# Fox attention pairs taken from the middle outwards, both score buffers in one pool, and the u and y transposes issued in halves

## The chip, the cores and the metric

The kernel runs on one core of one Trainium2 chip. The metric is device time in microseconds (us): the median of several executions. One more execution was taken with the hardware profiler, and every row below is from that one. TensorE is called PE (its weight loads PEld), VectorE DVE, ScalarE ACT, GpSimd POOL, and SP is the queue that issues most DMAs.

## The reference

Two residual layers over x [1, 2048, 1024] and a final RMSNorm, all float32. The part that the change touches most is the forgetting attention (FoX) of layer 0, eight heads of 64, in blocks of 128 queries:

```python
def one_block(args):
    i, qi, ci = args
    s = jnp.einsum('bhqd,bhkd->bhqk', qi, k, preferred_element_type=F32) * scale
    s = s + ci[..., :, None] - c[..., None, :]          # c = cumsum(log f)
    s = jnp.where(kpos[None, :] <= qpos[:, None], s, -jnp.inf)
    p = jax.nn.softmax(s, axis=-1)
    return jnp.einsum('bhqk,bhkd->bhqd', p.astype(v.dtype), v)
```

Around it, in each layer: `u = rmsnorm(h)`, `z = u @ w_in`, a second mixer (gated linear attention, GLA, in layer 0; retention and a dilated attention in layer 1), and `h + (mix * silu(gate)) @ w_out`.

## The kernel before

Nearly every product is done three times with float16 halves (high by high, high by low, low by high), so each operand is split into a high part (ACT, line 84) and a low part (DVE, line 85). The program runs through five stages.

1. **u** (0 to 130 us). For each of 16 tiles of 128 rows, `put_u` squares x on ACT with the junk result going into the low half of `u_x`, makes 1/rms (DVE, POOL), splits into `u_x` (two buffers), and one DMA transpose on SP writes both halves into `ut` (line 101). Beside it PE projects head 0.
2. **Fox** (130 to 1070 us). `periods` runs heads 0 to 7. While head h attends, PE is given the projection of head h+1 (`Heads.tiles`, four row tiles at a time, then one DMA transpose per quarter of the sequence, line 414) and other projections as fill; `merge` mixes both lists by cost, and `issue_after` keeps the value products behind the fill that was put ahead of them.
3. **Even mix** (1070 to 1372 us): `mix_out` with GLA recurrence beside it; it splits y and transposes it (line 322), multiplies by w_out, and makes u of the next layer.
4. **Dilated attention** (1372 to 2180 us).
5. **Odd mix** (2180 to 2489 us), with retention.

A pair step n of the Fox stage works on the query blocks 15-n and n, always 17 blocks of keys together. `scores` (lines 482 to 524): PE makes the scores in up to three PSUM tiles `big` (two buffers; lines 501 to 504), DVE adds the decay row `cb` and takes the maximum into `fx_s` (line 506), ACT takes the exponential in place (514) and copies the high half to `fx_ph` (518), DVE writes the low half back into `fx_s` (519), and SP issues two DMA transposes, `fx_ph` to `fx_th` (522) and `fx_s` to `fx_tl` (523). `values` follows two steps later (LAG): PE multiplies `fx_th` and `fx_tl` by v (533, 534), DVE scales (539), POOL adds the halves (545) and stores each group of four blocks (548). The last two value steps of a head run early in the next head's list. `decay` loads the two halves of `cb` per head by broadcast DMAs on SP (478) into three buffers, and POOL scales them (479).

`fx_s` has two buffers, one in the Fox pool for even n and one in the pool `wq` of the projection weights for odd n; when `start_gla` closes that pool during head 7, a single one is left (lines 485 and 486). The pool of the GLA is opened on the space of `wq`.

All engines run their queues in order. The framework writes the order of the queues at build time from its own estimate (line 1215) and puts in every wait.

Of the kernel before, what the change touches and what calls it, by code (L numbers as in the profile page):

```python
# [7 lines left out]
F32 = mybir.dt.float32  # L8
# [28 lines left out]
class Core:  # L37
# [52 lines left out]
    def put_u(self, u, t, h, work):  # L90

        nc = self.nc
        b, j = divmod(t, 4)
        if j == 0:
            u[b] = self.upool.tile([128, 2, KT, 512], F16, name="ut")
        x = work.tile([128, 2, D], F16, name="u_x", bufs=U_BUFS)
        ssq = self.small.tile([128, 1], F32, name="ssq")
        nc.scalar.activation(x[:, 1].bitcast(BF16), h, AF.Square, accum_out=ssq)
        r = self.rstd(ssq, D, 10)
        self.split(x[:, 0], x[:, 1], h, r[:, 0:1])  # L100
        nc.sync.dma_start_transpose(u[b].rearrange("p s k n -> p (s k) n")[:, :, j * 128:(j + 1) * 128],
                                    x.rearrange("p s n -> p (s n)"))
# [51 lines left out]
    def rows(self, out, u, t, w, c0, c1):  # L154
# [3 lines left out]
        uh, ul = u[b][:, 0], u[b][:, 1]  # L158
# [7 lines left out]
    def cols(self, out, u, b, w, c0, c1):  # L166

        nc = self.nc
        uh, ul = u[b][:, 0], u[b][:, 1]
# [120 lines left out]
def mix_out(co, work, inputs, h_d, gate_d, gate_k, kept_d, first, ws, recur, finish, lag):  # L290
# [13 lines left out]
    def prep(t):  # L304
# [8 lines left out]
        x = inputs.tile([128, 2, D], F16, name="u_x", bufs=U_BUFS)  # L313
        hi, lo = x[:, 0], x[:, 1]
# [6 lines left out]
        yt = work.tile([128, 2, KT, 128], F16, name="yt", bufs=lag + 1)  # L321
        nc.sync.dma_start_transpose(yt.rearrange("p s k n -> p (s k) n"), x.rearrange("p s n -> p (s n)"))
        ys[t] = (yt[:, 0], yt[:, 1], inv, h)
# [32 lines left out]
class Heads:  # L356
# [5 lines left out]
    def __init__(self, co, pools, xpool, wpool, u, w_in, col0, gain, chunked, rope=None):  # L362
# [4 lines left out]
        self.wpool_closed = False  # L367
# [95 lines left out]
def fox(co, work, heads, cum_d, mix_d, causal):  # L463
# [18 lines left out]
    def scores(h, n):  # L482

        st, f, cb = heads.st[h], heads.f[h], cbs[h]
        pool = work if n % 2 == 0 or heads.wpool_closed else heads.wpool
        raw = pool.tile([128, 2 * W], F16, name="fx_s", bufs=1)
# [29 lines left out]
        ph = work.tile([128, W], F16, name="fx_ph")  # L516
# [9 lines left out]
    def values(h, n):  # L526
# [11 lines left out]
        o2 = work.tile([128, 2, 128], F32, name="fx_o2")  # L538
        nc.vector.tensor_mul(o2, pv, nm[:, 6:8, None].to_broadcast([128, 2, 128]))  # L539
        for part, i in enumerate((15 - n, n)):  # L540
            g = i // 4
            if (h, g) not in outs:
                outs[h, g] = [work.tile([128, 4, 64], F32, name="fx_o", bufs=3), 0]
# [123 lines left out]
def gla(co, work, glq_d, glv_d, tables, gm):  # L667
# [307 lines left out]
def decoder(tc, cst, x, norm_even, w_in_even, b_f_even, w_lr_even, b_lr_even, gla_norm_even, w_out_even,  # L975
            norm_odd, w_in_odd, ret_gn_w_odd, ret_gn_b_odd, w_out_odd, final_norm, out):
    nc = tc.nc
    with ExitStack() as ctx:
# [240 lines left out]
```

## Time and profile before

| | |
|---|---|
| median of 3 runs | 2489.22 us (2487.48 to 2505.09) |
| the profiled execution's own time | 2491.33 us |
| its span, first to last instruction | 2489.5 us |
| TensorE busy, share of the span | 2231.9 us, 90% |
| DVE, ACT, POOL busy | 1562.9, 1122.8, 535.1 us |
| mean granted TensorE clock | 0.938 of full |

The median of the runs and the profiled execution differ by 0.1%. The page of the profile gives shares over the whole span; the stages have different limits, so waits are read stage by stage. A clock of 1.0 is the 2.4 GHz level, 0.5 the 1.2 GHz level.

### The profile page before, as it was taken

The numbers are of one execution on the slowest core, as the hardware profiler recorded it, in microseconds if no ns is written. First come the engines' busy times: TensorE is split into PE (matmuls) and PEld (weight loads), VectorE is DVE, ScalarE is ACT, GpSimd is POOL, SyncE is SP. The second block draws the span as 40 slices with busy tenths as digits, with TensorE's granted clock in tenths as the row PEclk, the third lists the DMA queues.
The fourth block names the chain that finished last, engine by engine and source line by source line (L and its number), as shares of the span: only waits on it lengthen the run. The fifth ranks groups of instructions, "written<-read, shape, count | busy, mean of one in ns | idle before, by whom it ended". The sixth has DMA issues, their size and how long they took to land. (4 is left out here: it accounts for less than half of the span.)

```text
span 2489.5 us, 51410 instructions
## 1 busy us (share of the span) xinstructions
PE 2231.9 (90%) x19956; PEld 1717.4 (69%) x19956; DVE 1562.9 (63%) x4870; ACT 1122.8 (45%) x2580; POOL 535.1 (21%) x638
## 2 busy tenths in 40 slices
PE   4888789998898898768989999999998999889998
PEld 3777678576687787534445898898887888765554
DVE  5346557576575665445554866666665757688764
ACT  5445445454444443334343555455554545533332
POOL 0021221201112112111111222212312222154441
PEclk8799899999999999869999999999999999989999
DMA  9848787888787756568776677886858667866553
GB/s 198 182 102 151 142 153 151 149 147 154 144 165 139 144 115 149 106 192 186 202 182 160 143 152 144 134 156 143 172 113 149 148 136 153 162 212 180 167 155 102
DMA packets 838452, 381.85 MB, mean 153 GB/s; under 512 B 741040, under 2 KB 797248, under 8 KB 837952
## 3 DMA queue, kind: packets, MB, share of 16 engines
q1 hardware_dynamic: 740784, 259.28, 53.9%
q0 software_dynamic: 23584, 82.33, 11.8%
q10 hardware_dynamic: 73840, 36.97, 6.0%
q8 instruction: 156, 2.56, 0.4%
q14 instruction: 88, 0.72, 0.1%
HBM read 135.40 MB, written 73.73 MB: 84 GB/s over the span
## 5 line engine op out<-in xcount | busy, mean ns | idle before, releaser
L162 PE MATMUL dn<-w,ut 128*128 128x192 f16 (+1 forms) x3840 | 1014.4, 264 | 24.8 <-DMA ut<-u_x 10.0
L163 PE MATMUL dn<-w,ut 128*128 128x192 f16 (+1 forms) x3840 | 1013.3, 264 | 0.0
L164 PE MATMUL dn<-w,ut 128*128 128x192 f16 (+1 forms) x3840 | 1012.6, 264 | 0.0
L162 PEld LDWEIGHTS <-ut 128*128 128x128 f16 x3968 | 395.6, 100 | 65.5 <-DMA ut<-u_x 29.3
L163 PEld LDWEIGHTS <-ut 128*128 128x128 f16 x3968 | 395.0, 100 | 39.3 <-issue 10.4
L164 PEld LDWEIGHTS <-ut 128*128 128x128 f16 x3968 | 394.8, 100 | 27.3 <-issue 1.4
L506 DVE CUSTOM_DVE_ANT_0 fx_s<-big,cb,hd_f 128x1024 f32<-128x1024 f32 (+7 forms) x128 | 134.1, 1048 | 173.7 <-DMA fx_tl<-fx_s 90.3
L514 ACT ACTIVATE fx_s<-fx_s,fx_nm 128x2048 f32<-128x2048 f32 (+15 forms) x128 | 152.7, 1194 | 194.0 <-DVE fx_nm L512 193.9
L897 ACT ACTIVATE dl_s<-dl_s,dl_m 128x256 f32<-128x256 f32 (+1 forms) x384 | 172.6, 451 | 107.0 <-DVE dl_m L896 93.0
L519 DVE TENSOR_TENSOR fx_s<-fx_s,fx_ph 128x2176 f16<-128x2176 f32 x64 | 155.0, 2422 | 38.4 <-ACT fx_ph L518 38.3
L501 PE MATMUL big<-head 128*128 128x512 f16 (+3 forms) x320 | 119.1, 372 | 59.9 <-DMA head<-qk_x 36.8
L893 DVE CUSTOM_DVE_ANT_0 dl_s<-big,dl_mask,hd_f 128x256 f32<-128x256 f32 (+1 forms) x384 | 141.5, 421 | 47.6 <-PE big L891 46.7
L79 POOL TENSOR_TENSOR rs_r<-rs_v,mhalf 128x1 f32<-128x1 f32 (+2 forms) x96 | 69.5, 727 | 427.4 <-DVE rs_v L76 407.0
L900 DVE TENSOR_TENSOR dl_pl<-dl_s,dl_ph 128x512 f16<-128x512 f32 (+2 forms) x96 | 101.4, 1058 | 66.2 <-ACT dl_ph L899 44.0
L533 PE MATMUL aux<-head,fx_th 128*128 128x128 f16 x1088 | 115.3, 227 | 25.0 <-DMA fx_th<-fx_ph 25.0
L85 DVE SCALAR_TENSOR_TENSOR w<-w_raw,w_gs,w 128x256 f16<-128x256 f32 (+2 forms) x296 | 123.1, 472 | 14.7 <-ACT w L84 14.5
L518 ACT ACTIVATE fx_ph<-fx_s 128x2176 f16<-128x2176 f32 x64 | 128.8, 2012 | 5.3 <-issue 3.3
L891 PE MATMUL big<-head 128*128 128x256 f16 (+1 forms) x384 | 129.7, 357 | 0.9 <-DMA head<-qk_x 0.9
L890 PE MATMUL big<-head 128*128 128x256 f16 (+1 forms) x384 | 129.6, 355 | 0.6 <-DVE dl_rec L893 0.6
L84 ACT ACTIVATE w<-w_raw,w_gs 128x256 f16<-128x256 f32 (+2 forms) x296 | 113.6, 466 | 32.8 <-DVE w_gs L143 24.0
L545 POOL TENSOR_TENSOR fx_o<-fx_o 128x64 f32<-128x64 f32 x128 | 52.9, 433 | 344.7 <-DVE fx_o L539 211.6
L534 PE MATMUL aux<-head,fx_tl 128*128 128x64 f16 x1088 | 110.1, 199 | 16.0 <-DMA fx_tl<-fx_s 15.9
(235 smaller groups left out, 4387.0 us busy)
## 6 DMA issues: line engine op xcount, KB each, us to landing
gate_d<-x_out POOLq DMA_DIRECT2D x64, 256.0 KB, 4.4
o_gate<-gate_d SPq DMA_DIRECT2D x32, 512.0 KB, 5.2
rec_d<-dl_rec POOLq DMA_DIRECT2D x16, 528.0 KB, 4.7
dl_rec<-rec_d POOLq DMA_DIRECT2D x16, 528.0 KB, 5.9
x_h<-in_x_dram SPq DMA_DIRECT2D x16, 512.0 KB, 4.8
cb<-cum_d SPq DMA_DIRECT2D x16, 512.0 KB, 9.5
o_mix<-mix_d SPq DMA_DIRECT2D x32, 256.0 KB, 2.8
o_h<-in_x_dram SPq DMA_DIRECT2D x16, 512.0 KB, 5.1
```

Of the source, the lines that this page charges most:

```text
L85: self.nc.vector.scalar_tensor_tensor(lo, x, scale, hi, op0=OP.mult, op1=OP.subtract)
L162: nc.tensor.matmul(out, uh[:, k, xs], wh[:, k, c0:c1], start=k == 0, stop=False)
L163: nc.tensor.matmul(out, uh[:, k, xs], wl[:, k, c0:c1], start=False, stop=False)
L164: self.last = nc.tensor.matmul(out, ul[:, k, xs], wh[:, k, c0:c1], start=False, stop=k == KT - 1)
L506: nc.vector.tensor_tensor_reduce(out=x[:, at + c * 1024:at + c * 1024 + wide], in0=p[:, :wide], in1=cb[c][:, :wide], scale=f[:, 0:1], scal ...
L514: nc.scalar.activation(x[:, sp], x[:, sp], AF.Exp, bias=nm[:, part:part + 1], accum_out=nm[:, 2 + part:3 + part])
L518: nc.scalar.activation(ph, x[:, 0:W], AF.Copy)
L519: nc.vector.tensor_sub(pl, x[:, 0:W], ph)
L890: nc.tensor.matmul(p[:, sp], st[:, 0, qs], st[:, 1, ks], start=True, stop=False)
L891: nc.tensor.matmul(p[:, sp], st[:, 0, qs], st[:, 2, ks], start=False, stop=True)
L893: nc.vector.tensor_tensor_reduce(out=raw[:, sp], in0=p[:, sp], in1=mask[:, 256 - 128 * len(vs):], scale=f[:, 0:1], scalar=-3.0e38, op0=OP. ...
L897: nc.scalar.activation(raw[:, sp], raw[:, sp], AF.Exp, bias=m[:, i:i + 1], accum_out=rec[:, n, 65:66])
```

## The change

Four things. Fox pairs are taken from n = 7 to n = 0, so the first pair of a head is (8, 7) and the last (15, 0). Both `fx_s` buffers are in the Fox pool for the whole stage; to make room `fx_ph` and `fx_o2` go from two buffers to one, `fx_o` from three to two, and the GLA's `gl_ek` from four to three. The high and low halves of u, and of y, are tiles of their own, each with a DMA transpose of its own (twice as many, half as wide). The query and key transposes of a head's quarter (line 414) stay one DMA, as before.

```diff
@@ put_u @@
-            u[b] = self.upool.tile([128, 2, KT, 512], F16, name="ut")
-        x = work.tile([128, 2, D], F16, name="u_x", bufs=U_BUFS)
+            u[b] = (self.upool.tile([128, KT, 512], F16, name="uh"),
+                    self.upool.tile([128, KT, 512], F16, name="ul"))
+        hi = work.tile([128, D], F16, name="u_hi", bufs=U_BUFS)
+        lo = work.tile([128, D], F16, name="u_lo", bufs=U_BUFS)
...
-        nc.sync.dma_start_transpose(u[b].rearrange("p s k n -> p (s k) n")[:, :, j * 128:(j + 1) * 128],
-                                    x.rearrange("p s n -> p (s n)"))
+        for part, x in zip(u[b], (hi, lo)):
+            nc.sync.dma_start_transpose(part[:, :, j * 128:(j + 1) * 128], x)
@@ mix_out, prep @@
-        yt = work.tile([128, 2, KT, 128], F16, name="yt", bufs=lag + 1)
-        nc.sync.dma_start_transpose(yt.rearrange("p s k n -> p (s k) n"), x.rearrange("p s n -> p (s n)"))
+        yh = work.tile([128, KT, 128], F16, name="yh", bufs=lag + 1)
+        yl = work.tile([128, KT, 128], F16, name="yl", bufs=lag + 1)
+        nc.sync.dma_start_transpose(yh, hi)
+        nc.sync.dma_start_transpose(yl, lo)
@@ fox @@
-        pool = work if n % 2 == 0 or heads.wpool_closed else heads.wpool
-        raw = pool.tile([128, 2 * W], F16, name="fx_s", bufs=1)
+        raw = work.tile([128, 2 * W], F16, name="fx_s")
...
-        ph = work.tile([128, W], F16, name="fx_ph")
+        ph = work.tile([128, W], F16, name="fx_ph", bufs=1)
...
-        o2 = work.tile([128, 2, 128], F32, name="fx_o2")
+        o2 = work.tile([128, 2, 128], F32, name="fx_o2", bufs=1)
...
-                outs[h, g] = [work.tile([128, 4, 64], F32, name="fx_o", bufs=3), 0]
+                outs[h, g] = [work.tile([128, 4, 64], F32, name="fx_o", bufs=2), 0]
...
-        steps = [(1.9, lambda n=n: scores(h, n), 1.5, lambda n=n: behind(h, n)) for n in range(8)]
+        steps = [(1.9, lambda n=n: scores(h, n), 1.5, lambda n=n: behind(h, n)) for n in range(7, -1, -1)]
@@ gla @@
-                ek = work.tile([128, 128], F32, name="gl_ek", bufs=4)
+                ek = work.tile([128, 128], F32, name="gl_ek", bufs=3)
```

## Rows read from the trace of the kernel before

**Rows 1.** The page's first line: the span.

```profile
span 2489.5 us, 51410 instructions
```

**Rows 2.** Busy time by stretch (start:end, length, then busy us of PE, PEld, DVE, ACT, POOL with instruction counts, granted clock, DMA share, GB/s): the Fox stage, the even mix, the dilated stage.

```profile
170.00:1070.00 900.00, 796.85 (x8027) 638.09 (x8026) 557.02 (x1292) 411.51 (x664) 165.82 (x240) 0.94 0.75 144
1110.00:1372.00 262.00, 238.66 (x1250) 124.84 (x1248) 141.83 (x435) 104.94 (x275) 36.57 (x58) 0.95 0.73 180
1372.00:2180.00 808.00, 771.47 (x7844) 682.64 (x7842) 547.49 (x2270) 419.51 (x1288) 192.67 (x206) 0.97 0.75 147
```

**Rows 3.** What PE waited for from 130 to 1070 us: us in total, times, longest.

```profile
PE big L501 <- DMA head<-qk_x: 36.8, 6, 9.4
PE aux L533 <- DMA fx_th<-fx_ph: 25.0, 7, 5.8
...
PE aux L534 <- DMA fx_tl<-fx_s: 15.9, 13, 3.2
```

**Rows 4.** Timeline of PE: the first score product of heads 4, 5 and 7 (three of the six waits); start, us, engine, line, shape, count, and in brackets the idle time before it and its releaser.

```profile
569.98 0.61 PE L501 MATMUL big<-head 128*128 128x512 f16 x1 [9.38 <-DMA head<-qk_x]
670.65 0.61 PE L501 MATMUL big<-head 128*128 128x512 f16 x1 [6.74 <-DMA head<-qk_x]
872.46 0.61 PE L501 MATMUL big<-head 128*128 128x512 f16 x1 [5.78 <-DMA head<-qk_x]
```

**Rows 5.** Busy time by stretch, the sum line over the six stretches of half clock that follow or span the six waits (360.4 to 367.3, 466.2 to 469.7, 565.2 to 575.5, 667.6 to 674.5, 766.6 to 773.4, 869 to 875.8 us).

```profile
sum 41.20, PE 25.24 PEld 10.05 DVE 11.27 ACT 0.00 POOL 12.47; mean PE 4.21 PEld 1.68 DVE 1.88 ACT 0.00 POOL 2.08
```

**Rows 6.** DVE: its waits for the score buffer from 130 to 1070 us, and on its timeline the first reduction of the second pair of heads 2, 3, 6 and 7.

```profile
DVE fx_s L506 <- DMA fx_tl<-fx_s: 90.3, 23, 9.7
...
374.37 1.28 DVE L506 CUSTOM_DVE_ANT_0 fx_s<-big,cb,hd_f 128x1024 f32<-128x1024 f32 x1 [3.50 <-DMA fx_tl<-fx_s]
478.16 1.28 DVE L506 CUSTOM_DVE_ANT_0 fx_s<-big,cb,hd_f 128x1024 f32<-128x1024 f32 x1 [5.52 <-DMA fx_tl<-fx_s]
783.56 1.28 DVE L506 CUSTOM_DVE_ANT_0 fx_s<-big,cb,hd_f 128x1024 f32<-128x1024 f32 x1 [5.45 <-DMA fx_tl<-fx_s]
888.65 1.28 DVE L506 CUSTOM_DVE_ANT_0 fx_s<-big,cb,hd_f 128x1024 f32<-128x1024 f32 x1
```

**Rows 7.** Timeline of the SP queue where head 1 ends and head 2 begins (the second number is the time that the issue took).

```profile
346.76 0.36 SPq L478 DMA_DIRECT2D cb<-cum_d  x1
347.30 7.72 SPq L522 DMA_TRANSPOSE fx_th<-fx_ph  x1
355.12 3.11 SPq L523 DMA_TRANSPOSE fx_tl<-fx_s  x1
...
359.84 0.90 SPq L478 DMA_DIRECT2D cb<-cum_d  x1
360.90 8.73 SPq L522 DMA_TRANSPOSE fx_th<-fx_ph  x1
369.73 2.39 SPq L523 DMA_TRANSPOSE fx_tl<-fx_s  x1
```

**Rows 8.** Where head 0 ends and head 1 begins: two copies to `fx_ph` on ACT's timeline, and two first value products on PE's.

```profile
252.17 2.00 ACT L518 ACTIVATE fx_ph<-fx_s 128x2176 f16<-128x2176 f32 x1
265.13 2.02 ACT L518 ACTIVATE fx_ph<-fx_s 128x2176 f16<-128x2176 f32 x1
...
255.99 0.29 PE L533 MATMUL aux<-head,fx_th 128*128 128x128 f16 x1 [5.45 <-DMA fx_th<-fx_ph]
271.25 0.23 PE L533 MATMUL aux<-head,fx_th 128*128 128x128 f16 x1 [3.87 <-DMA fx_th<-fx_ph]
```

**Rows 9.** The last pair of head 7: its first reduction on DVE's timeline, its first value product on PE's.

```profile
1043.51 1.28 DVE L506 CUSTOM_DVE_ANT_0 fx_s<-big,cb,hd_f 128x1024 f32<-128x1024 f32 x1 [6.04 <-DMA fx_tl<-fx_s]
...
1059.19 0.29 PE L533 MATMUL aux<-head,fx_th 128*128 128x128 f16 x1 [5.76 <-DMA fx_th<-fx_ph]
```

**Rows 10.** DMA transposes: issue time on SP (ns, shortest/median/longest, first and last start) of u (2048 columns; the first stage alone) and of the dilated stage (512 to 1024 columns), then the median us from issue to landing of the same two.

```profile
L101 SPq DMA_TRANSPOSE ut<-u_x x16: 1317/2612/4720, 13.5 to 105.3; - x16
...
L901 SPq DMA_TRANSPOSE dl_pt<-dl_ph x96: 1188/1232/3942, 1402.7 to 2159.8; - x96
...
dl_pt<-dl_ph SPq DMA_TRANSPOSE x96, 3.6
...
ut<-u_x SPq DMA_TRANSPOSE x32, 4.4
```

**Rows 11.** The u stage: PE's waits for transposed u (0 to 170 us), busy time of two stretches, and the projections' matmuls over the whole run (ns, first and last start).

```profile
PE aux L162 <- DMA ut<-u_x: 13.8, 7, 3.5
PE dn L162 <- DMA ut<-u_x: 10.0, 3, 3.7
...
0.00:107.00 107.00, 65.06 (x727) 54.57 (x728) 55.68 (x162) 53.52 (x101) 9.00 (x20) 0.81 0.95 202
107.00:130.00 23.00, 23.00 (x225) 19.45 (x222) 8.93 (x24) 12.67 (x21) 1.65 (x2) 0.93 0.50 99
...
L162 PE MATMUL dn<-w,ut x3840: 242/264/421, 17.9 to 2211.1; 128*128 128x192 f16 x106, 128*128 128x256 f16 x86
```

**Rows 12.** From Fox to the even mix: DVE's wait for weights of the next layer, the first read-back of a mixed tile on SP, and the stores of Fox outputs on POOL (ns, first and last start).

```profile
DVE w_am L131 <- DMA w_raw<-in_w_in_odd_dram: 10.3, 1, 10.3
...
1067.02 0.32 SPq L301 DMA_DIRECT2D o_mix<-mix_d  x1
...
L548 POOL DMA_DIRECT2D mix_d<-fx_o x32: 750/767/825, 225.3 to 1066.9; - x32
```

More of the change, by code (lines that the diff above doesn't have):

```diff
@@ L94, in put_u @@
         if j == 0:
-            u[b] = self.upool.tile([128, 2, KT, 512], F16, name="ut")
-        x = work.tile([128, 2, D], F16, name="u_x", bufs=U_BUFS)
+            u[b] = (self.upool.tile([128, KT, 512], F16, name="uh"),
+                    self.upool.tile([128, KT, 512], F16, name="ul"))
+        hi = work.tile([128, D], F16, name="u_hi", bufs=U_BUFS)
+        lo = work.tile([128, D], F16, name="u_lo", bufs=U_BUFS)
         ssq = self.small.tile([128, 1], F32, name="ssq")
-        nc.scalar.activation(x[:, 1].bitcast(BF16), h, AF.Square, accum_out=ssq)
+        nc.scalar.activation(lo.bitcast(BF16), h, AF.Square, accum_out=ssq)
         r = self.rstd(ssq, D, 10)
-        self.split(x[:, 0], x[:, 1], h, r[:, 0:1])
-        nc.sync.dma_start_transpose(u[b].rearrange("p s k n -> p (s k) n")[:, :, j * 128:(j + 1) * 128],
-                                    x.rearrange("p s n -> p (s n)"))
+        self.split(hi, lo, h, r[:, 0:1])
+        for part, x in zip(u[b], (hi, lo)):
+            nc.sync.dma_start_transpose(part[:, :, j * 128:(j + 1) * 128], x)
     def begin_w(self, into, key, *args):
@@ L157, in rows @@
         b, j = divmod(t, 4)
-        uh, ul = u[b][:, 0], u[b][:, 1]
+        uh, ul = u[b]
         wh, wl = w[0], w[1]
@@ L168, in cols @@
         nc = self.nc
-        uh, ul = u[b][:, 0], u[b][:, 1]
+        uh, ul = u[b]
         wh, wl = w[0], w[1]
@@ L312, in prep @@
                                            gate_k[:, c:c + 1], y[:, cs], op0=OP.mult, op1=OP.mult)
-        x = inputs.tile([128, 2, D], F16, name="u_x", bufs=U_BUFS)
-        hi, lo = x[:, 0], x[:, 1]
+        hi = inputs.tile([128, D], F16, name="u_hi", bufs=U_BUFS)
+        lo = inputs.tile([128, D], F16, name="u_lo", bufs=U_BUFS)
         ssq = co.small.tile([128, 1], F32, name="ssq")
@@ L320, in prep @@
         co.split(hi, lo, y, s)
-        yt = work.tile([128, 2, KT, 128], F16, name="yt", bufs=lag + 1)
-        nc.sync.dma_start_transpose(yt.rearrange("p s k n -> p (s k) n"), x.rearrange("p s n -> p (s n)"))
-        ys[t] = (yt[:, 0], yt[:, 1], inv, h)
+        yh = work.tile([128, KT, 128], F16, name="yh", bufs=lag + 1)
+        yl = work.tile([128, KT, 128], F16, name="yl", bufs=lag + 1)
+        nc.sync.dma_start_transpose(yh, hi)
+        nc.sync.dma_start_transpose(yl, lo)
+        ys[t] = (yh, yl, inv, h)
     def products(t):
@@ L366, in __init__ @@
         self.w, self.x, self.st, self.v, self.f = {}, {}, {}, {}, {}
-        self.wpool_closed = False
     def space(self, h):
@@ L1084, in start_gla @@
             close(wq)
-            heads.wpool_closed = True
             recur.append(opened("gl", 2, "right"))
```

## The prediction

> **What bounds the kernel now.** I began with the busy time by stretch [rows 2]. PE is busy for 797 of 900 us in the Fox stage, 239 of 262 in the even mix and 771 of 808 in the dilated stage. PE is the bound everywhere, and only time in which it stands still or runs at half clock can be won. The change adds and removes no product, so I looked next at PE's list of waits, stage by stage. In the Fox stage the largest entry is the query and key transposes of the next head, 36.8 us in six waits, then 25.0 and 15.9 us for the transposed probabilities [rows 3]. The timeline of PE puts the six at the head boundaries [rows 4]: the first pair of a head is (15, 0), which needs the last quarter of queries and keys, and that quarter is projected last. The granted clock then shows a second price: stretches at half clock, 41.2 us together, with PE busy for 25.24 us in them [rows 5]. At full clock this work takes half, so 12.6 us more belong to the six waits, 49.4 us in all.
>
> The DVE list is the warning. DVE waits 90.3 us, 23 times, for the score buffer, that is for the low-half transpose of the pair two steps back [rows 6]. So the chain DVE, ACT, DVE, SP, transpose runs close to PE, and a PE that comes earlier may only wait at the next place.
>
> **Order of the pairs.** It removes the need for the last quarter from the first four pairs of a head; widths, number of reductions and bytes are unchanged, because every pair has 17 blocks. That a wait for one quarter is not a wait for the whole tile is seen in the u stage, where the first projection runs at 17.9 us while transposes into the same u tile are issued later, the last of the stage at 105.3 us [rows 10, 11]. Upper bound: all 49.4 us. What is late next? At the boundary SP first issues a broadcast load of `cb`, and the transposes behind it take 7.72 and 8.73 us to issue against 3.11 and 2.39 us for their neighbours [rows 7]. So the last pair of the old head gives back its score buffer late, and the second pair of the new head cannot start its reductions before. For heads 2, 3 and 6 that reduction already starts on this landing, after 3.50, 5.52 and 5.45 us of idle DVE [rows 6]. PE's later score products need the PSUM tile that this reduction frees, so there I count nothing as won. For head 7 the same reduction waits for nothing [rows 6], and I count the whole gap and its mean share of slow clock (12.6/6 = 2.1): 5.8 + 2.1 = 7.9 us. For heads 4 and 5 the trace does not tell how much lies between; I take half of 9.38 + 6.74 + 2 x 2.1 = 20.3 [rows 4], 10.2 us. Sum -18.1, bounds 0 and -49.4. I stay nearer to the low end because of head 1. Its boundary never had the wait for queries and keys, and PE stood there for 5.45 and 3.87 us on the transposed probabilities [rows 8].
>
> **Both score buffers in the Fox pool.** Before `start_gla` this is two buffers in both kernels and changes nothing. After it one buffer becomes two. The last pair of head 7 now waits 6.04 us for the only buffer, and PE ends the stage with 5.76 us of waiting for that pair's transpose [rows 9]. With a second buffer the pair starts up to 6.0 us earlier. I take -5.8, bounds 0 (another wait ends last) and -6.0.
>
> **One `fx_ph` buffer.** This adds a wait: the ACT copy of a pair must wait until the previous pair's transpose has landed. Behind it on ACT are the evictions of PE's projections, which have two PSUM buffers. The copies are some 13 us apart [rows 8], the copy takes 2.0 us and a transpose of about this size, as u's, 4.4 us to land [rows 10], so in mid-head the wait is covered. At the boundaries it is not: the copies of 252.17 and 265.13 us are 13.0 us apart, but the first one's transpose let PE go only at 271.25 us [rows 8]. The second copy would have waited 6.1 us. The low half's transpose is queued on SP behind the `cb` load anyway [rows 7], so most of this delay falls into time that is already lost, and PE has a projection unit in hand (5.2 us in the kernel's own cost list, line 259). I take +4, bounds 0 and +43 (seven boundaries at 6.1 us).
>
> **u and y in halves.** In the u stage PE waits 13.8 + 10.0 us for transposed u in ten waits [rows 11]. A transpose of 1024 columns or fewer lands in 3.6 us against 4.4 us for 2048 [rows 10], and the high half can leave one DVE split earlier. I count 1 us for each of ten waits, 10 us at most. But the DMA engines are 0.95 busy up to 107 us, and from 107 to 130 us PE is busy in 23.00 of 23.00 us [rows 11], so what comes earlier mostly joins a queue. On the other side, two halves strictly one after the other would take 2 x 3.6 = 7.2 us against 4.4, so 2.8 us more for each of 16 tiles, 45 us. But an issue takes 1.2 us against a landing of 3.6 us [rows 10], so the second half is under way while the first is in flight, and I stay near the gain: -3, bounds +45 and -10. SP's issue time rises little: two at 1.23 us against one at 2.61 us in this stage [rows 10], and SP has nothing urgent behind them. In both mixes I cost the halves at nothing: PE is the cover, at 239 of 262 us in the even one [rows 2]; without it the price is one more issue of 1.2 us for each tile.
>
> The Trainium skill (DMA: Bandwidth & Descriptors, Rules for kernel authors) wants transfers merged, ideally 1 MiB each, and its section on latency speaks of a fixed cost near 2 us for each DMA. By that figure, charged in series, the 16 added transposes of the u stage would cost an estimated 32 us instead of winning 3, which is rival 4 below. No row here shows a fixed cost alone.
>
> **Smaller edits.** One `fx_o2` and two `fx_o` buffers: POOL's adds and stores follow within a step, so nothing, unless POOL is held by a `cb` load (up to +3). Three `gl_ek` buffers: nothing, up to +3 if ACT waits for PE's transpose. The new last pair holds blocks 15 and 0, so the mix must read rows 0 to 127 back after the stage's last store. It now issues this load at 1067.02 us, and the last store is issued at 1066.9 us [rows 12]. Waiting for its landing delays SP by some 4 us, with the next loads of the mix behind it. The cover is DVE's wait of 10.3 us for weights [rows 12], which holds back the first use of this tile. So nothing, and up to +5 without the cover.
>
> **Sum.** -18.1 - 5.8 + 4 - 3 = -22.9. The profiled execution's own time is 2491.33 us, 1.8 us over its span [rows 1] and 2.1 us over the median; so 2491.3 - 22.9 = 2468.4, or 2466 on the scale of the median.
>
> **Rivals.**
> 1. *The next wait takes the whole gain.* PE meets the late transposes at every boundary, as at head 1, and only the tail is won: about -6 to -10, so 2482. For it: rows 6 and 8. Against it: head 7.
> 2. *The whole price comes back.* The framework rewrites the order of the queues, and could put enough projection work where PE would wait: -49.4 - 5.8 + 3, so 2437. Against it: the 25.0 and 15.9 us of other waits [rows 3].
> 3. *Slower: one `fx_ph` buffer stops ACT.* Place: the seven head boundaries. Price: up to 6.1 us each [rows 8], 43 us, with nothing won at the boundaries and 9 us elsewhere: +34, so 2523. It decides if ACT's stop is longer than the projection that PE has in hand, some 5 us.
> 4. *Each transpose has a price of its own.* The two halves follow one another in the u stage without overlap: 45 us for 16 tiles, against -22.9 + 3 from the rest, so 2514. It decides if the halves don't overlap while u is late for PE. Against it: PE is the cover from 107 us on [rows 11].
> 5. *The change doesn't do what it says*, if quarters were not told apart; rows 10 and 11 all but exclude it, and I give it no share.
>
> **How the numbers follow.** Forecast (2446 to 2481) 0.45; rival 1 0.25; rival 2 0.15; rival 3 0.10; rival 4 0.05. The range must reach rival 2's middle on one side and stop short of rival 3 on the other: 2438 to 2502. A measurement of this kernel tells about 1%, 25 us, from no change, so faster means below 2464: rival 2 and nearly half of the forecast, 0.37. Slower means above 2514: most of rival 3 with a little more, 0.10. The rest, 0.53, lies within 1%.
>
> **What would show it.** In the profile after, PE's list has no wait of a first score product for `head`; its six half-clock stretches at the boundaries shrink; waits for `fx_th`, `fx_tl` or DVE's `fx_m` grow by some 30 us there. DVE's wait of 6.04 us before the last pair is gone. ACT's copy into `fx_ph` shows waits for DMA `fx_th`, a few us at boundaries alone. PE's ten waits for u are fewer or shorter. The dilated stage keeps its 808 us within 1%. I am wrong if PE's total of waits in the Fox stage stays where it is, if copies into `fx_ph` wait in mid-head too, or if a stage that the change hardly touches moves by more than 10 us because the framework has ordered its queues anew.

## The result

The changed kernel takes 2423.82 us in the median of four runs (2417.69 to 2428.66), against 2491.14 us for the kernel before in the same rounds. The ratio is 0.972, interval 0.967 to 0.976. The forecast was 2466 us, the range 2438 to 2502: the change is 42 us faster than forecast and lies below the range. Two more measurements of it gave ratios of 0.969 (0.965 to 0.973) and 0.968 (0.964 to 0.972).

Busy time by stretch of the kernel after, cut at the points at which the stages meet (columns as in [rows 2]): to the first reduction; heads 0 to 6; head 7; the end of Fox to the first mix product; the even mix; its end to the first dilated score; the dilated stage; its end to the odd mix; the odd mix.

```profile
span 2426.9 us, 51567 instructions
0.00:165.90 165.90, 114.24 (x1260) 97.64 (x1261) 81.81 (x223) 80.38 (x142) 16.04 (x27) 0.88 0.80 168
165.90:883.90 718.00, 630.11 (x6501) 507.04 (x6501) 447.82 (x1050) 333.99 (x517) 123.97 (x187) 0.94 0.81 147
883.90:1023.90 140.00, 131.94 (x1323) 110.42 (x1323) 94.67 (x209) 66.57 (x123) 25.40 (x44) 0.98 0.65 151
1023.90:1045.70 21.80, 21.80 (x180) 18.17 (x178) 12.34 (x40) 9.74 (x20) 5.67 (x9) 0.95 0.85 229
1045.70:1291.70 246.00, 237.19 (x1201) 118.49 (x1200) 151.91 (x469) 112.09 (x305) 36.41 (x57) 0.99 0.87 210
1291.70:1308.00 16.30, 16.30 (x198) 16.13 (x195) 12.26 (x38) 6.11 (x15) 2.62 (x4) 1.00 0.66 156
1308.00:2131.70 823.70, 771.90 (x7787) 680.78 (x7786) 545.95 (x2252) 417.06 (x1279) 195.65 (x207) 0.96 0.74 142
2131.70:2180.20 48.50, 42.63 (x294) 32.88 (x293) 36.79 (x97) 16.99 (x36) 22.87 (x22) 0.82 0.78 242
2180.20:2418.20 238.00, 235.98 (x1225) 123.03 (x1224) 165.03 (x494) 77.29 (x143) 99.09 (x81) 0.98 0.56 162
```

The same stretches of the kernel before, cut at the same points of its own trace:

```profile
0.00:169.50 169.50, 116.53 (x1244) 100.23 (x1245) 81.42 (x218) 80.04 (x140) 15.36 (x27) 0.87 0.75 164
169.50:874.40 704.90, 627.74 (x6481) 500.70 (x6481) 449.31 (x1051) 333.32 (x511) 132.65 (x189) 0.95 0.80 149
874.40:1064.60 190.20, 165.56 (x1532) 135.96 (x1530) 106.07 (x236) 77.07 (x149) 31.57 (x48) 0.91 0.56 124
1064.60:1095.70 31.10, 12.39 (x49) 7.39 (x48) 14.34 (x48) 9.05 (x31) 4.25 (x8) 0.50 0.62 190
1095.70:1354.30 258.60, 237.69 (x1157) 117.14 (x1156) 137.17 (x418) 102.25 (x267) 34.60 (x55) 0.95 0.76 186
1354.30:1378.90 24.60, 22.17 (x246) 21.54 (x245) 18.90 (x66) 10.49 (x27) 4.19 (x6) 0.93 0.46 97
1378.90:2177.80 798.90, 762.37 (x7740) 673.77 (x7738) 538.95 (x2234) 414.44 (x1274) 189.42 (x203) 0.97 0.76 148
2177.80:2226.30 48.50, 41.88 (x295) 32.41 (x291) 39.73 (x106) 17.67 (x37) 25.92 (x23) 0.84 0.75 241
2226.30:2480.80 254.50, 245.13 (x1223) 128.28 (x1224) 174.69 (x494) 77.34 (x143) 96.65 (x81) 0.94 0.52 151
```

Read the second column of both. The span is 62.6 us shorter: head 7 gives 50.2, the odd mix 16.5, the even mix 12.6, the two joins (the stretches on either side of the even mix) 9.3 and 8.3, the start 3.6. Heads 0 to 6, where the forecast had most of its gain, are 13.1 us *longer*, and the dilated stage is 24.8 us longer. In head 7 and the join behind it, PE goes from 165.56 of 190.2 and 12.39 of 31.1 us (half clock) to 131.94 of 140.0 and 21.80 of 21.8 us.

The products are the same in both kernels, 19956 matmuls, so a stage can also get shorter because its work is done elsewhere. From head 7 to the first dilated score there are 82 matmuls fewer after (2902 against 2984); the start, heads 0 to 6 and the dilated stage hold 16, 20 and 47 more. Over the whole span PE is busy for 2202.5 us instead of 2231.9, at a mean granted clock of 0.953 instead of 0.938: 29 of the 62.6 us are matmuls that took less time, 33 are time in which PE no longer stands.

PE's waits from 130 us to the end of Fox, after; this answers [rows 3]:

```profile
PE big L503 <- DVE fx_m L508: 65.3, 23, 7.8
PE aux L536 <- DMA fx_tl<-fx_s: 19.5, 6, 7.3
PE aux L535 <- DMA fx_th<-fx_ph: 11.4, 3, 4.5
```

The wait for the next head's queries and keys, 36.8 us before, is gone. The wait for DVE's maximum stands in its place. And ACT has the wait that one `fx_ph` adds, in total and at its longest place, 44 us after the first reduction of head 4, so in mid-head:

```profile
ACT fx_ph L520 <- DMA fx_th<-fx_ph: 20.3, 10, 3.8
...
603.49 2.02 ACT L520 ACTIVATE fx_ph<-fx_s 128x2176 f16<-128x2176 f32 x1 [3.79 <-DMA fx_th<-fx_ph]
```

### The profile page after: what moved, and what is told of

It reads as the page before. It is cut to its first block, busy times and chain, and to the rows that moved or that the text cites. A ratio compares the mean times of both kernels' runs of the same rounds, so it can differ in the third digit from the quotient of the medians.

```text
span 2426.9 us, 51567 instructions
## 1 busy us (share of the span) xinstructions
PE 2202.5 (91%) x19956; PEld 1704.6 (70%) x19956; DVE 1550.9 (64%) x4870; ACT 1121.4 (46%) x2580; POOL 528.3 (22%) x638
## 4 chain that ended last, share of the span: by engine, by line
PE 55%; DMA 16%; DVE 9%; issue 4%; ACT 2%; SPq 2%; POOL 1%; ACTq 0%; DVEq 0%; POOLq 0%
PE dn L164 9%; PE dn L165 9%; PE dn L166 9%; DMA fx_tl<-fx_s 4%; PE dn L335 3%; PE dn L337 3%; PE dn L336 3%; DMA dl_pt<-dl_pl 3%; PE big L892 2%; PE big L893 2%; DMA gl_x<-glq_d 2%; DVE fx_s L508 2%; PE aux L535 2%; PE big L503 2%; PE big L504 1%
## 5 line engine op out<-in xcount | busy, mean ns | idle before, releaser
L164 PE MATMUL dn<-w,uh 128*128 128x192 f16 (+1 forms) x3840 | 1015.2, 264 | 16.1 <-DMA uh<-u_hi 7.2
L166 PE MATMUL dn<-w,ul 128*128 128x192 f16 (+1 forms) x3840 | 1014.0, 264 | 4.8 <-DMA ul<-u_lo 4.8
L165 PE MATMUL dn<-w,uh 128*128 128x192 f16 (+1 forms) x3840 | 1014.5, 264 | 0.0
L164 PEld LDWEIGHTS <-uh 128*128 128x128 f16 x3968 | 396.3, 101 | 58.8 <-DMA uh<-u_hi 16.5
L166 PEld LDWEIGHTS <-ul 128*128 128x128 f16 x3968 | 394.0, 100 | 43.8 <-DMA ul<-u_lo 15.1
L165 PEld LDWEIGHTS <-uh 128*128 128x128 f16 x3968 | 395.6, 100 | 31.8 <-issue 2.2
L516 ACT ACTIVATE fx_s<-fx_s,fx_nm 128x1152 f32<-128x1152 f32 (+15 forms) x128 | 152.7, 1194 | 207.3 <-DVE fx_nm L514 196.2
L520 ACT ACTIVATE fx_ph<-fx_s 128x2176 f16<-128x2176 f32 x64 | 128.8, 2012 | 25.1 <-DMA fx_th<-fx_ph 20.3
L547 POOL TENSOR_TENSOR fx_o<-fx_o 128x64 f32<-128x64 f32 x128 | 41.9, 347 | 364.0 <-DVE fx_o L541 183.6
```

What stands on the lines that cost most here:

```text
L164: nc.tensor.matmul(out, uh[:, k, xs], wh[:, k, c0:c1], start=k == 0, stop=False)
L165: nc.tensor.matmul(out, uh[:, k, xs], wl[:, k, c0:c1], start=False, stop=False)
L166: self.last = nc.tensor.matmul(out, ul[:, k, xs], wh[:, k, c0:c1], start=False, stop=k == KT - 1)
L516: nc.scalar.activation(x[:, sp], x[:, sp], AF.Exp, bias=nm[:, part:part + 1], accum_out=nm[:, 2 + part:3 + part])
```

## The experiments

Times by stage of every profiled run, in us, cut as above (the join from the dilated stage to the odd mix, 45 to 52 us in all of them, is left out). "Same" is the kernel before run and profiled a second time. A row is one profiled execution and need not lie near its kernel's median: it took 2466.30 us in e5 (median 2482.84), 2459.43 in e6 (2478.69), 2470.03 in e8 (2481.72), 2407.85 in e13 (2426.32) and 2509.22 in e3 (2491.43). The ratio is from all executions.

| kernel | start | heads 0-6 | head 7 | join | even mix | join | dilated | odd mix | ratio (95%) |
|---|---|---|---|---|---|---|---|---|---|
| before | 169.5 | 704.9 | 190.2 | 31.2 | 258.5 | 24.7 | 798.9 | 254.5 | 1 |
| e7 same | 173.4 | 710.9 | 192.2 | 32.4 | 261.6 | 23.3 | 816.3 | 254.2 | one run |
| e1 order | 171.4 | 690.0 | 170.9 | 32.8 | 259.1 | 24.6 | 807.9 | 255.6 | 0.987 (0.983-0.991) |
| e2 pool | 168.8 | 717.7 | 144.0 | 21.1 | 261.9 | 24.4 | 826.2 | 247.7 | 0.985 (0.980-0.990) |
| e3 halves | 166.4 | 721.4 | 191.6 | 25.4 | 251.5 | 17.8 | 828.6 | 243.6 | 0.996 (0.993-0.998) |
| e4 order, pool | 169.7 | 719.0 | 138.6 | 21.6 | 255.2 | 24.9 | 815.4 | 250.8 | 0.978 (0.973-0.983) |
| e5 one buffer | 169.9 | 712.5 | 157.0 | 31.7 | 251.0 | 22.0 | 813.7 | 252.1 | 0.991 (0.988-0.995) |
| e6 one ph | 170.4 | 711.1 | 174.2 | 23.8 | 254.5 | 23.3 | 805.5 | 239.1 | 0.989 (0.984-0.994) |
| e8 y | 168.4 | 702.6 | 187.9 | 27.1 | 258.7 | 24.4 | 799.4 | 239.9 | 0.993 (0.990-0.996) |
| e10 order, one ph | 168.9 | 707.8 | 171.7 | 25.9 | 254.7 | 24.6 | 816.4 | 238.9 | 0.987 (0.983-0.990) |
| e14 order, out | 167.0 | 691.5 | 168.8 | 32.0 | 257.3 | 24.9 | 815.5 | 253.3 | 0.985 (0.981-0.988) |
| after | 165.9 | 718.0 | 140.0 | 21.7 | 246.0 | 16.3 | 823.7 | 238.0 | 0.972 (0.967-0.976) |
| e11 after | 165.0 | 716.7 | 139.2 | 20.6 | 250.5 | 16.3 | 818.3 | 236.2 | 0.969 (0.965-0.973) |
| e15 after | 165.2 | 719.8 | 139.7 | 21.0 | 247.4 | 16.3 | 824.8 | 240.2 | 0.968 (0.964-0.972) |
| e12 cb | 170.3 | 725.4 | 140.4 | 20.8 | 248.7 | 16.3 | 827.3 | 241.5 | 0.971 (0.967-0.976) |
| e9 two ph | 168.6 | 699.3 | 141.0 | 21.1 | 247.4 | 16.3 | 823.7 | 242.3 | 0.962 (0.958-0.966) |
| e16 two ph | 167.3 | 700.7 | 140.6 | 21.0 | 249.8 | 16.3 | 812.1 | 243.8 | 0.960 (0.955-0.964) |
| e13 two out | 170.2 | 698.0 | 139.0 | 21.0 | 246.2 | 16.3 | 814.9 | 244.7 | 0.969 (0.964-0.974) |

**How far a stage moves by itself (e7).** The kernel before, unchanged.

> The kernel before once more, for a second profile of the same program: it shows how far a stage moves by itself. Theory: heads 0 to 6 and head 7 within 4 us (704.9, 190.2), both mixes within 4 us, the dilated stage within 15 us (798.9). If the dilated stage moves by under 3 us, the 9 to 27 us that it took more in the other kernels come from the change.

Its second profile has a span of 2518.6 us, 29 us more than the first: heads 0 to 6 +6, the dilated stage +17.4, the mixes +3 and 0. The expectation had 4 us for the heads and 15 for the dilated stage, and both were exceeded a little. So the 24.8 us that the dilated stage seems to lose can't be told from the kernel's own spread: it takes 799 to 816 us in the two profiles of before and 818 to 825 in the three of after. A small part of it is work that came from elsewhere: before the first dilated score, the join held 240 projections of the next layer in the kernel before and holds 192 after, and the others run in the dilated stage. 192 take 16.3 us there, so the 48 are worth an estimated 4 us, and as much of the join's 8.3 us is no gain.

**The parts alone (e1 to e4).** e1 is the line of the pairs:

```diff
-        steps = [(1.9, lambda n=n: scores(h, n), 1.5, lambda n=n: behind(h, n)) for n in range(8)]
+        steps = [(1.9, lambda n=n: scores(h, n), 1.5, lambda n=n: behind(h, n)) for n in range(7, -1, -1)]
```

> The kernel before with the pairs taken from n = 7 to n = 0 and nothing else. Order theory (the recorded rival 2: the waits for query and key transposes and their slow clock come back whole): 40 to 50 us faster, 2440 to 2450, with heads 0 to 6 shorter by some 45 us than their 704.9 us. Next-wait theory (rival 1): the six waits for head are gone, waits for the PSUM score tile and the transposed probabilities grow by as much, heads 0 to 6 within 10 us of 704.9, total within 10 us of before.

e2 is the pool with its smaller buffer counts:

```diff
-        pool = work if n % 2 == 0 or heads.wpool_closed else heads.wpool
-        raw = pool.tile([128, 2 * W], F16, name="fx_s", bufs=1)
+        raw = work.tile([128, 2 * W], F16, name="fx_s")
...
-        ph = work.tile([128, W], F16, name="fx_ph")
+        ph = work.tile([128, W], F16, name="fx_ph", bufs=1)
...
```

> The kernel before with both score buffers in the Fox pool and the smaller buffer counts that make room, order and transposes as before. Pool theory: the single score buffer after the closing of the weight pool made the last four pairs of head 7 run one after the other, and PE spent on them the projections that are kept for the change to the mix; two buffers win 50 to 80 us between 874 and 1379 us of before, total 2415 to 2440. Recorded step (only the last wait of 6 us): 2 to 6 us faster, and up to 43 us slower if one fx_ph buffer stops ACT.

e3 is the halves of u and y (the first two parts of the diff of the change):

> The kernel before with u and y in halves, each with its own transpose, nothing else. Halves theory (they shorten both mixes, which lost 12.5 and 16.5 us in the changed kernel): 25 to 35 us faster, the odd mix 12 to 17 us shorter. Recorded step: about 3 us faster in the u stage and nothing in the mixes. Rival 4 (each transpose has a price): u stage 45 us longer.

e4 is e1 and e2 together:

> Order and pool together, transposes whole. If the parts add up: the sum of the two runs alone. Pool theory with the next-wait theory: 2420 to 2440, and heads 0 to 6 some 10 us longer than before, as in the changed kernel (718.0 against 704.9 us), the cost of one fx_ph buffer. If the halves carry a third of the gain: 2445 to 2455.

By their ratios to before (2504.94 us in these rounds), order, pool and halves win 33, 38 and 11 us, and order and pool together 55, less than the 71 of their sum. The pool, forecast at 5.8 less 4, is the largest part. In the stages it is head 7 (190.2 to 144.0 us) and the join behind it (31.2 to 21.1). The order is worth 15 us in heads 0 to 6, near the forecast, and 19 in head 7, which was not forecast. With the pool change beside it (e4), the 15 us in heads 0 to 6 are gone.

The expectations came out in part. e1 lies between its two theories, which had given heads 0 to 6 some 45 us or under 10. e2 won 53 us from head 7 to the first dilated score, as its pool theory had it, but only 38 in all, since heads 0 to 6 and the dilated stage grew. e3 won 11 us where 25 to 35 were expected.

**What in the pool change shortens head 7 (e5, e6).** e5 has the smaller buffer counts of e2 and frees the space of the odd buffer too, but keeps a single one from `start_gla` on:

```diff
-        pool = work if n % 2 == 0 or heads.wpool_closed else heads.wpool
-        raw = pool.tile([128, 2 * W], F16, name="fx_s", bufs=1)
+        odd = n % 2 and not heads.wpool_closed
+        raw = work.tile([128, 2 * W], F16, name="fx_s1" if odd else "fx_s0", bufs=1)
...
```

> The kernel before, its odd fx_s moved into the Fox pool (and the smaller buffer counts that make room for it), but from start_gla on only one of the two is used, as before. The GLA's space is thus free early, and the end of head 7 still has a single score buffer. Theory A, the late start of the GLA is the price: head 7 takes 140 to 150 us as in e2_pool (144.0), the gap to the first mix product 21 us, the time is that of e2_pool, 0.985 of before. Theory B, the single buffer is the price: head 7 stays at 180 to 190 us, and with the 13 us that one fx_ph costs in heads 0 to 6 the ratio is 1.000 to 1.005, whatever the GLA does. If both count: head 7 at 160 to 175 us, ratio 0.990 to 0.997.

e6 is the kernel before with one `fx_ph`:

```diff
-        ph = work.tile([128, W], F16, name="fx_ph")
+        ph = work.tile([128, W], F16, name="fx_ph", bufs=1)
```

> The kernel before with one fx_ph buffer instead of two and nothing else. Theory: ACT's copy waits for the transpose, 25 us in all at the head boundaries, heads 0 to 6 take 715 to 720 us instead of 705, ratio 1.003 to 1.008. Prediction's term: +4 us, ratio 1.000 to 1.002. Rival: the cost of one fx_ph arises only where pairs of the new order crowd the boundary; then ACT waits under 10 us and the ratio is 1.000.

e5 came out at 157.0 us for head 7, between theory A and the case in which both count, so neither theory alone holds; its ratio, 0.991, is the one given for both together. The load of the GLA's first inputs (count, ns, first and last start) of before, then of e5, shows the first half of it: the GLA's pool lies on the space of `wq`, and as long as the odd `fx_s` lies there, the GLA's loads start 94 us into head 7. In e5 they start 14 us ahead of head 7. The other kernels divide in the same way: 84 to 99 us into head 7 in all eight that keep the odd `fx_s` on `wq`, 14 to 17 us ahead of it in the ten that don't.

```profile
L678 SPq DMA_DIRECT2D gl_x<-glq_d x11: 518/529/700, 968.6 to 1099.1; - x11
...
L678 SPq DMA_DIRECT2D gl_x<-glq_d x13: 518/538/1305, 868.0 to 1098.2; - x13
```

e6 was a surprise: with a buffer less and nothing else it is faster than before (0.989), which none of its three theories had. Head 7 took 174.2 us although the GLA's loads still start 85 us into it. The timeline of DVE shows a place that differs. First before, then e6: the reduction of weights `w_am`, which waits for a DMA, and the first reduction of the seventh pair:

```profile
1016.03 2.29 DVE L131 TENSOR_REDUCE w_am<-w_raw 128x8 f32<-128x2048 f32 x1 [9.13 <-DMA w_raw<-in_w_out_even_dram]
1019.25 1.28 DVE L506 CUSTOM_DVE_ANT_0 fx_s<-big,cb,hd_f 128x1024 f32<-128x1024 f32 x1 [0.94 <-PE big L502]
...
1013.45 1.28 DVE L506 CUSTOM_DVE_ANT_0 fx_s<-big,cb,hd_f 128x1024 f32<-128x1024 f32 x1
1014.66 2.28 DVE L131 TENSOR_REDUCE w_am<-w_raw 128x8 f32<-128x2048 f32 x1
```

In before, DVE stands 9.13 us at `w_am` with the reduction queued behind it. In e6 the framework has put the reduction first, and it starts 131.9 us behind the head's first reduction instead of 144.9. The four kernels with the long head 7 (before, e7, e3, e8: 188 to 192 us) all stand 4 to 9 us at this place; e1, e6, e10 and e14 (169 to 174) stand there at most 2.3 us. The length of the stop does not decide (e3 has 4.2 us and the long head), and no run moved this instruction alone. So head 7 falls from 190 to about 172 us where the queue is ordered otherwise, to 157 where the GLA also starts early (e5), and to 144 with the second buffer (e2). Each of the three shows at a place of its own. These are the times from one pair's first reduction to the next one's, read from DVE's timeline in head 7, in us:

| kernel | GLA's loads | pair 5 to 6 | pair 6 to 7 | pair 7 to 8 |
|---|---|---|---|---|
| before | late | 42.6 | 33.3 | 24.2 |
| e7 same | late | 43.8 | 32.8 | 23.9 |
| e6 one ph | late | 39.8 | 24.7 | 19.7 |
| e5 one buffer | early | 29.9 | 23.6 | 20.3 |
| e2 pool | early | 27.8 | 21.4 | 6.1 |

Before and its repeat differ by 1.2 us at most. The queue's order is the step from 33 to 25 us at pair 6 to 7. The GLA's start is the step from 40 to 30 at pair 5 to 6 (with the new order of the pairs from 43.5 in e1 to 18.9 in e4). The second buffer is the step from 20 to 6 at pair 7 to 8, where the wait for the only buffer goes. The last pair's first reduction in e5, then in e2:

```profile
1020.88 1.28 DVE L506 CUSTOM_DVE_ANT_0 fx_s<-big,cb,hd_f 128x1024 f32<-128x1024 f32 x1 [5.24 <-DMA fx_tl<-fx_s]
...
1006.17 1.27 DVE L504 CUSTOM_DVE_ANT_0 fx_s<-big,cb,hd_f 128x1024 f32<-128x1024 f32 x1
```

The join behind head 7 stays at 31.7 us in e5 and takes 21.1 with the second buffer; the other kernels with one buffer have 23.8 to 32.8 us.

**What one `fx_ph` costs (e6, e10, e9, e15, e16).** e6 alone takes 711.1 us in heads 0 to 6, between the two profiles of before (704.9, 710.9), although ACT waits 22.2 us for `fx_th` there. e10 is e6 with the order of e1:

> Two edits of the kernel before: pairs from n = 7 to 0, and one fx_ph buffer instead of two; the score buffers stay where they were. Theory, PE's wait for the next head's queries and keys was the cover of ACT's stop, and the new order takes the cover away: heads 0 to 6 take 712 to 722 us, against 690.0 with the order alone and 711.1 with one fx_ph alone, so the order's 15 to 20 us are lost. Rival, both are independent: 690 + 0 to 6 = 690 to 697 us. Second rival, the pool change and not fx_ph costs those 29 us: also 690 to 697 us.

It takes 707.8 us, so the order's gain is lost: the theory is right in kind, its bounds 4 us too high, and both rivals with 690 to 697 fall. Heads 0 to 6 by stretch of e1 and of e10:

```profile
171.40:861.40 690.00, 619.58 (x6473) 497.73 (x6473) 448.26 (x1046) 332.34 (x509) 125.61 (x186) 0.96 0.83 151
168.90:876.70 707.80, 631.53 (x6473) 507.11 (x6473) 447.82 (x1046) 332.53 (x509) 120.56 (x186) 0.94 0.81 147
```

PE runs the same 6473 matmuls. 12.0 of the 17.8 us are matmuls that take longer at a lower granted clock (0.94 against 0.96), 5.8 are standing time. The loss is seen in this stage alone: the whole kernels have the same ratio (0.987), because e10's odd mix and the join behind head 7 came out 16.7 and 6.9 us shorter. e9 gives the changed kernel a second `fx_ph` for heads 0 to 6, on the space of `wq`, where it doesn't hold up the GLA:

```diff
-        ph = work.tile([128, W], F16, name="fx_ph", bufs=1)
+        pool = heads.wpool if n % 2 and h < 7 and not heads.wpool_closed else work
+        ph = pool.tile([128, W], F16, name="fx_ph", bufs=1)
...
```

> The changed kernel with a second fx_ph buffer for odd pairs of heads 0 to 6, on the space of the projection weights (4.3 KB for each partition), and a single one in head 7. Theory, one fx_ph ate the gain of the order: ACT's 20 us of waits in heads 0 to 6 go, these heads take 690 to 700 us instead of 718, head 7 and the transition stay at 140 and 22 us, time 2400 to 2410 us on the scale of before at 2491, ratio 0.963 to 0.967. Rival, DVE's waits for cb bound these heads: they stay at 712 to 718 us, ratio 0.970 to 0.973. Second rival, the odd buffer delays the GLA again: head 7 grows by over 10 us.

> The changed kernel on the same chip as e16_two_ph, in the same rounds. Theory, the second fx_ph wins the 18 us that the profiles show in heads 0 to 6: this kernel's ratio to before is 0.007 above that of e16_two_ph, about 0.969 against 0.962. Rival, the difference between the two came from the chips on which they ran: the ratios agree within 0.002.

> The kernel of e9_two_ph on the same chip as e15_after, in the same rounds. Theory: 0.962, 0.007 below e15_after. Rival: within 0.002 of e15_after; then the 18 us that heads 0 to 6 win are given back elsewhere.

Heads 0 to 6 fall from 718.0 to 699.3 us, and the GLA keeps its early start. In the same rounds on one chip the changed kernel takes 2427.67 us and the one with the second buffer 2408.54: ratios 0.968 and 0.960, a difference of 19 us where the stage had shown 18.7. The executions of the two don't overlap (2417.51 to 2438.05 and 2396.28 to 2416.72 us), so this version is faster than the changed kernel. e11, the changed kernel once more, was not on e9's chip, so the comparison that it was meant for is that of e15 and e16. It repeated its stages within its bounds, and its ratio, 0.969, is 0.001 below them:

> The changed kernel once more, on the chip of e9_two_ph. Theory: 0.970 to 0.974 of before, so e9_two_ph with its 0.962 is about 1% faster; heads 0 to 6 within 6 us of 718.0, head 7 within 3 us of 140.0, both mixes within 5 us of 246.0 and 238.0, the dilated stage within 18 us of 823.7. If it comes out at 0.962 too, the second fx_ph won nothing.

**What else holds heads 0 to 6 (e12 to e14).** e12 is the changed kernel with a fourth `cb` buffer:

> The changed kernel (one fx_ph) with a fourth cb buffer: the second half of an odd head's decay row, heads 0 to 6, lies on the space of the projection weights. In the changed kernel DVE waits 31.3 us in seven times for POOL's cb at the head boundaries. Theory, the late cb is a bound of its own beside fx_ph: DVE's wait for cb falls below 15 us, heads 0 to 6 take 700 to 710 us instead of 718, ratio 0.962 to 0.966. Rival, the stop of ACT for the single fx_ph ends last at the boundary: heads 0 to 6 stay within 4 us of 718, ratio 0.969 to 0.972, and DVE's wait for cb turns into one for fx_tl or PE's for fx_th.

DVE's wait for `cb` falls from 31.3 to 10.1 us and its wait for `fx_tl` rises from 77.6 to 85.4. After, then e12, both from 165 to 885 us:

```profile
DVE fx_s L508 <- DMA fx_tl<-fx_s: 77.6, 19, 8.9
...
DVE fx_s L508 <- POOL cb L482: 31.3, 7, 8.0
...
DVE fx_s L509 <- DMA fx_tl<-fx_s: 85.4, 19, 13.8
...
DVE fx_s L509 <- POOL cb L483: 10.1, 2, 5.6
```

The heads get no shorter, so `cb` was not what ended last. The rival has the ratio right (0.971), but not the stage: 725.4 us are 7 above 718, where it allowed 4. e14 tries the smaller output buffers with the new order, e13 gives them back in e9:

> Two edits of the kernel before: pairs from n = 7 to 0, and the smaller output buffers (one fx_o2, two fx_o); fx_ph keeps two buffers and the score buffers stay where they were. Theory, the output buffers cost about 9 us in the new order: heads 0 to 6 take 696 to 702 us instead of 690.0, ratio 0.990 to 0.992. Rival, they cost nothing, as the prediction has it: 688 to 693 us, ratio 0.985 to 0.989.

> The kernel of e9_two_ph with, beside the second fx_ph, a second fx_o2 (odd pairs) and a third fx_o (the group of blocks 0 to 3) for heads 0 to 5, on the space of the projection weights. Theory, single fx_o2 and two fx_o hold POOL and through it DVE, and cost the 9 us by which e9_two_ph (699.3) stands above the order alone (690.0): heads 0 to 6 take 688 to 694 us, ratio 0.957 to 0.960. Rival, the 9 us come from the pool's rearranged queues: heads 0 to 6 stay at 696 to 702, ratio 0.961 to 0.964. Second rival, tiles that the old heads leave late on that space delay the next weights or the GLA: slower than e9_two_ph.

In these heads they cost nothing: 691.5 us against 690.0, and 698.0 against 699.3. Nor is the difference of 9.3 us between e9 and e1 all loss, since e9 does more in these heads:

```profile
168.60:867.90 699.30, 629.34 (x6501) 506.14 (x6501) 450.17 (x1050) 334.24 (x517) 129.34 (x187) 0.95 0.83 151
```

PE has 28 more matmuls there than in e1 and is busy 9.8 us longer. They are projections that no longer have to be done later. The 10 us by which the changed kernel (718.0) and e4 (719.0) stand above e10 are not explained.

e13 as a whole was a miss. Its ratio is 0.969 (0.964 to 0.974) where 0.957 to 0.964 was expected, against 0.962 for e9 and 0.960 for e16, which ran on e13's chip at another time. Its stages look as good as theirs because its profiled execution is the shortest of its four. So its second rival, that it is slower than e9, is not excluded, and what would make it so no row shows.

**The halves in the mixes (e3, e8).** e8 halves only the transposes of y:

> The kernel before with only the transpose of y, in both mixes, issued in two halves into tiles of their own; u is as before. Theory, the halves of y start the next layer's u and the dilated stage earlier: from the last mix product to the first dilated score 16 to 18 us instead of 24.7, the even mix 8 us shorter than 258.5. Rival, that gain comes from the halves of u, which share the path from the mix to the dilated scores: 24 us stay there. For the odd mix: if halving y is what shortens it, it takes 243 us or less instead of 254.5; if a new order of the queues does it, any value from 239 to 256 may come, and it is 254 if the order stays as before.

The even mix and the join to the dilated stage stay as they were (258.7 and 24.4 us), so the halves of y alone do not shorten them. The join is short only with the halves of u: it takes 16.3 to 17.8 us in all eight kernels with u and y in halves and 22.0 to 24.9 in the ten with u whole. The halves of u alone were not tried. For the even mix the times say less: e3 has 251.5 us, but so has e5 with u whole (251.0). The odd mix falls to 239.9 us, and this too is not y: e6 and e10, whose y is transposed in one piece, have 239.1 and 238.9. PE's waits there, before and e6:

```profile
PE big L822 <- DVE rt_am L816: 9.3, 4, 3.0
...
PE big L822 <- DVE rt_am L816: 2.8, 3, 1.5
...
2209.90:2449.00 239.10, 235.14 (x1223) 121.93 (x1224) 167.08 (x494) 77.16 (x143) 95.27 (x81) 0.99 0.56 161
```

The last line is the whole odd mix of e6. e7, e5, e2 and e4 have PE's and DVE's queues of the odd mix in the order of before, and 254, 252, 248 and 251 us. Where the order is another, it takes 236 to 256 us, mostly 238 to 245. The granted clock goes from 0.94 to 0.99 as the short waits vanish, and PE's busy time for the same 1223 matmuls from 245.13 to 235.14 us.

## Why the prediction was wrong

The sum had -22.9 us and -67.3 was measured (2423.82 against 2491.14). By the runs of the parts the pool is worth 38, the order 33 and the halves 11 us, and they don't add.

**The bound of the pool step failed.** "Before `start_gla` this is two buffers in both kernels and changes nothing" looked at who uses the buffer, not at what lies on its space. The bound of 6.0 us was the one visible wait of the last pair [rows 9]. What ran late behind it, the GLA's start, has no wait of its own in PE's list, because PE had projections to do instead: 1000 of the 1532 matmuls of head 7 in before were projections, against 822 of 1323 after. At the join none were left, and PE ran 12.39 of 31.1 us at half clock; after, 144 projections fill it. This part belongs to the single buffer and not to the GLA's start: e5, with the early start, has 24 projections in the join and 31.7 us, e2 has 119 and 21.1. Measured: head 7 and join together -56.3 in e2 (e5: -32.7 without the second buffer), where the sum had -5.8. So the second buffer, the one part that the step had counted, is worth 23.6 and not 5.8. Some 16 to 19 of the 56.3 us come with another order of the queues, as e1, e6 and e10 have it too; the stop at `w_am` is where the trace shows it, but no run moved that instruction alone.

**The order was right alone and lost in company.** -18.1 stands against -14.9 in e1, or -20.9 against the second profile of before. The wait for `head` went, and PE's wait for `fx_m` in heads 0 to 6 rose from 17.3 to 50.7 us, the growth of some 30 us that the prediction named. Before, then e1:

```profile
PE big L501 <- DVE fx_m L506: 17.3, 14, 6.3
...
PE big L501 <- DVE fx_m L506: 50.7, 18, 9.1
```

With the whole change PE stands for 101.8 us in heads 0 to 7 before and 96.0 after, so the sign that PE's total of waits stays where it is came nearly true.

What the prediction did not see is that the terms don't add. "Most of this delay falls into time that is already lost" was true of one `fx_ph` in the old order (e6: 0 to 6 us) and false in the new one (e10: 18). That PE's wait for `head` was the cover is my reading of e1, e6 and e10 together; no row shows it. The mis-sized term is +4, with +18 measured (e10 against e1; 18.7 for the changed kernel against e9). Nor was "in mid-head the wait is covered" true: of the 17.4 us of ACT's waits in heads 0 to 6 of after, four waits with 6.4 us lie 11 to 15 us behind a head's first reduction, and the two longest, 3.8 us each, in mid-head. So rival 3's mechanism came, at another place than it named and at under half of its price.

The trace of before could have told this. The prediction took u's 4.4 us for the landing and one gap of 13 us between copies. The transpose of `fx_ph` itself takes 5.8 us (median, from issue to landing):

```profile
fx_th<-fx_ph SPq DMA_TRANSPOSE x64, 5.8
```

The copies follow one another after 11.8 us in the median of heads 0 to 6, and 12 of the 63 next copies of before start ahead of the landing of the transpose before them, five of these in mid-head.

**The halves.** The u stage was forecast 3 us shorter. With the halves it takes 165.0 to 170.3 us, without them 167.0 to 173.4: a gain of that size, inside the spread. But PE's waits for u there did not get fewer or shorter, as forecast; they are 26.3 us in 16 waits after against 23.8 in ten before. Rival 4 is excluded: in no kernel is the stage 45 us longer, and a half lands in 3.8 and 3.4 us against 4.4 for the whole [rows 10]:

```profile
uh<-u_hi SPq DMA_TRANSPOSE x32, 3.8
ul<-u_lo SPq DMA_TRANSPOSE x32, 3.4
```

The rule of the Trainium skill (DMA: Bandwidth & Descriptors, Rules for kernel authors) is to coalesce many small transfers into one large one. For these transposes, of 256 KB a half, the trace shows no price of the split: the u stage takes 166.4 us in e3 against 169.5 and 173.4 in the two profiles of before.

"In both mixes I cost the halves at nothing" failed for the even mix: PE busy in 239 of 262 us is no cover for the other 23. Before, 19.1 us of them were waits for ACT's `gl_kd` of the GLA. In e8, with y alone in halves, it is 11.7, after 1.0:

```profile
PE aux L733 <- ACT gl_kd L716: 19.1, 9, 5.2
...
PE aux L735 <- ACT gl_kd L718: 11.7, 5, 3.1
...
PE aux L735 <- ACT gl_kd L718: 1.0, 2, 0.6
```

This wait is 11.7 to 19.1 us in all ten kernels with u whole and 0.2 to 1.0 in all eight with u and y in halves (0.2 in e3). So it goes with the halves of u, or of u and y together, and why ACT comes earlier stays open. The even mix after holds 44 more matmuls (1201 against 1157) in 12.6 us less. Nearly all of them are products of the GLA that before ran in head 7 and the join; it holds no projection of the next layer in either kernel.

**The framework's new order** stood among the signs that would make the prediction wrong, without a share of the sum. It moved the odd mix by up to 16 us (e6, e8, e10: edits that leave its instructions as they were, or split only its transposes) and head 7 by 16 (e6).

**The dilated stage** was to stay within 1%. Its two profiles of the same program differ by 2.2%, so that test could tell nothing.

**Slips of the working** that changed little: two issues at 1.23 us take less than one at 2.61, not a little more; rival 2's "+ 3" has no term behind it (with +4 and -3 it is +1, so 2435 us); and the range's 2438 stops just short of rival 2's middle. The measured 2423.82 is below that too.

## What to carry to other kernels

Before costing a buffer that moves, list what else lies on its space and when that may start: a stage that starts late need not show as a wait of the engine, if the engine has other work meanwhile, so a list of waits does not price it. Two terms that lie under the same wait must not be costed apart: take the wait away and ask each of the others again. Where a framework orders the queues itself, an edit may move a stage that it does not touch by 10 to 20 us, as here the odd mix and head 7; profile the kernel before twice and give this a share in the range.

## What the runs showed of the hardware

What a lost stretch of time costs in clock and what in standing differs from case to case, so neither column can be left out. In the odd mix of e6 against before, 10.0 of 15.4 us were the same 1223 matmuls at a mean granted clock of 0.94 instead of 0.99. In heads 0 to 6 it was 12.0 of 17.8 us in e10 against e1 (0.94 and 0.96), but 0.8 of 18.7 in the changed kernel against e9 (630.11 and 629.34 us busy for 6501 matmuls), and 5.4 of 19.1 when both were measured again (e15, e16). The clock also moves by itself: the even mix of before and of its repeat e7 had 237.7 and 243.5 us of busy PE, at 0.95 and 0.93.

A DMA transpose of half the width lands a little sooner and not in half the time: 3.8 and 3.4 us for the halves of u against 4.4 for the whole.
